# Hybrid decoder layer: one pipeline per kind of attention head beside the block products, operands fetched a head ahead, other homes for raw weights

## The chip, the core and the metric

The kernel runs on one core of a Trainium2 chip. The metric is the device time of one execution in microseconds; the time before is the median of 3 runs. The core's engines are named as in the profile: PE (TensorE matmul; PEld is its weight load), DVE (VectorE), ACT (ScalarE), POOL (GpSimd) and SP (SyncE, which here only issues DMAs). Each engine works through its own instructions in order and waits on semaphores for the others.

## The reference

One decoder layer over 512 tokens of width 2048, all in float32:

```python
h = rmsnorm(x, attn_pre_norm[l])
proj = h @ w_in
gq, gk, gv, gg, ga, dq, dk, dv = [proj[..., int(offs[i]):int(offs[i + 1])]
                                  for i in range(len(IN_SPLITS))]
log_a = jax.nn.log_sigmoid((ga @ w_alpha_up + b_alpha).astype(jnp.float32)) / GLA_TAU
o_a = gla_chunked(gq, gk, gv, log_a)
o_a = rmsnorm(o_a, gla_norm) * silu(gg)
o_b = diff_attention(dq, dk, dv, lam)
o_b = rmsnorm(o_b, diff_norm) * (1.0 - lambda_init)
m = jnp.concatenate([o_a, o_b], axis=-1) @ w_o
x = x + rmsnorm(m, attn_post_norm[l])
h = rmsnorm(x, ffn_pre_norm[l])
f = conv_ffn(h, w_ffn_in[l], conv_w[l], conv_b[l], w_ffn_out[l])
x = x + rmsnorm(f, ffn_post_norm[l])
```

(The shapes of the heads are left out.) There are 4 gated-linear-attention heads (GLA, keys 128 wide, values 256), whose forget gate goes through a product of rank 16, and 4 differential-attention heads (diff: two softmaxes over 128-wide queries and keys, the second subtracted, values 256 wide). Then come w_o and a gated MLP of width 5632 with a depthwise convolution.

## The kernel before

**Products.** Each float32 factor is split in a high half (fp32r) and a low rest: `granule` (L128) takes 4 x 128 rows by 256 columns of weights from `raw`, ACT copies the high half into `ring` (L137) and DVE subtracts it for the low half (L138). A product then takes three matmuls, high by high, high by low, low by high. The normalised input stands in SBUF as `ah` and `al`. `ring` has three slots; a slot's two halves lie at offsets from `place_w`: `APART` for turned units, `APART_N` for units that aren't turned. Here they differ in the low half:

```python
LEVEL, APART, APART_N = (0, 0), (16, 112), (112, 16)
```

**Input projection.** gv's first half, gq's and gk's first half are plain products (`proj_n`, L191 to L193, and `proj_t`, L173 to L175, 512 columns moving). The other columns go in ten units (`InUnit`), each a 2 x 2 block product that saves one of eight block products by adding blocks beforehand. A unit has seven segments x0, z0, y0, z1, x1, y1, y2, of two granules with 24 matmuls of 256 columns each, 336 in all; a turned unit (queries and keys) has the weights stationary (L695 to L697), the others (values, gates) have the sums stationary (L699 to L701). The left factors are blocks of the input (a11, a12, a22) and four sums of blocks (s5, s2, s3, s7) in two halves, which `in_sums` makes with 1024-wide DVE instructions (L402 to L418) and splits (ACT L150, DVE L151). s7 goes into the room of a block of `ah`/`al` that is no longer needed, so it is split only behind the last plain product. The raw weight blocks are added by accumulating DMAs on POOL's queue (`more`) or by DVE (L720). t, the block that x0 starts with, comes into `raw` (4 buffers); b22 comes into `wide` (2 buffers, shared with the sums' temporaries q and r).

**Attention beside it.** Heads are Python generators in the list `fill`. After each granule, `step()` takes `pace` steps of the first generator; what it issues there stands behind that granule's matmuls in PE's order. Each head is a generator of its own; it begins with its DMAs from DRAM, where the units put queries, keys and values. Diff heads have stages for each block of 128 queries: `probs` (scores L589, softmax on DVE and ACT L591 to L605), `turn` (transposes L612, copy aT L614), `values` (L620, norm L623 to L626), `store` (transposes L632, copy dst L634, DMA to `dstd`). A stage runs one block behind the one before it, and a head runs NT + 3 = 7 steps, so the pipeline empties at each head's end. What the heads wrote comes back as `dt` (`place_diff`, split at L150/L151) and, gated, as `ogt` (`turn_gate`, transposes L781) to be w_o's left factor. The forget gate (L422 to L466: load gar, split gas, products L439/L440, L448, Abs, Exp, Ln, scan) feeds the GLA heads.

**Order.** A scheduler sets each engine's order from the order of the program and the buffers, which is why a step that moves in the program moves on all engines. In the last unit `drain()` runs what is left of `fill` in one go:

```python
        else:
            drain()
            place_diff(0)
            u.x1()
```

Of the kernel before, what the change touches and what calls it, by code (L numbers as in the profile page):

```python
# [9 lines left out]
F32 = mybir.dt.float32  # L10
# [25 lines left out]
def hybrid_layer(ctx: ExitStack, tc: tile.TileContext, x, attn_pre_norm, w_in, w_alpha_up, b_alpha,  # L36
# [351 lines left out]

    s7raw = []

    def in_sums():
        for i in range(2):
            def blk(r, c):
                return [v[:, 2 * r + i, HK * c:HK * (c + 1), :].bitcast(F32) for v in (ah, al)]

            a11, a12, a21, a22 = blk(0, 0), blk(0, 1), blk(1, 0), blk(1, 1)

            def flat(name):
                return wide(name).rearrange("p (k c) -> p k c", c=P)
# [10 lines left out]
            yield  # L410
            tt(q, q, a12[0], ALU.add)
            tt(q, q, a12[1], ALU.add)
            split(sums["s3"][0][:, i], sums["s3"][1][:, i], q)
            yield
            r = flat("r")
            tt(r, a11[0], a21[0], ALU.subtract)
            tt(r, r, a11[1], ALU.add)
            tt(r, r, a21[1], ALU.subtract)  # L418
            s7raw.append(r)
            yield  # L420

    def forget_gate():  # L422
        gar = quarter("gar").rearrange("p (k r) -> p k r", r=RANK)
        dma(gar, w_in3[:, :, C_GA:C_GA + RANK])
# [12 lines left out]
        gav = gab[:80, :].rearrange("p (t c) -> p t c", c=P)  # L437
        for k in range(KT):
            mm(gav, gas[:, k, :], ah[:, :, k, :], start=k == 0, stop=False)  # L439
            mm(gav, gas[:, k, :], al[:, :, k, :], start=False, stop=k == KT - 1)  # L440
        gaT = block_tile("gaT")[:80, :]
        nc.vector.tensor_copy(gaT, gab[:80, :])
        yield

        za, bt = [], []
        for h in range(GH):
            zb = bank()
            mm(zb, wup[:, h * P:(h + 1) * P], gaT, start=True, stop=True)  # L448
            bcol = cols[:, h:h + 1]
            za.append(qk_tile("za"))  # L450
            bt.append(tmp("bt"))
            act(za[h], zb, AF.Abs, bias=bcol)
            ts(bt[h], zb, bcol, 0.0, ALU.add, ALU.min)
            if h % 2:
                yield
        for m in za:
            act(m, m, AF.Exp, scale=-1.0)
        for m in za:
            act(m, m, AF.Ln, bias=1.0)
        yield  # L460
        for h, m in enumerate(za):
            tt(m, bt[h], m, ALU.subtract)
            nc.vector.tensor_tensor_scan(bt[h], keep, m, 0.0, ALU.mult, ALU.add)
            dma(bcd[h], bt[h])
            if h % 2:
                yield  # L466


    def gla_head(h):
        q, k, b = (qk_tile(n) for n in ("gq", "gk", "gb"))  # L470
        dma(q, gqd[h // 2][:, h % 2, :])
        dma(k, gkd[h // 2][:, h % 2, :])
        dma(b, bcd[h])
# [4 lines left out]
        yield  # L478
        bc = b.rearrange("p (c x) -> p c x", c=4)
        v = "p (n x) -> p n x"  # L480
        sc = mx.tile([P, 4, P], F32, name="sc", tag="qk", bufs=4)
# [49 lines left out]
            nc.tensor.transpose(kb[:, c * P:(c + 1) * P], kd[:, c * P:(c + 1) * P], ident)  # L531
        kT = tmp("kT")
        act(kT[:, :3 * P], kb[:, :3 * P], AF.Copy)
        yield
        st = None
        for c in range(4):
# [22 lines left out]


    SC = DQK ** -0.5
    dd = []

    def diff_head(h):
        if not dd:
            dist = mx.tile([P, S], F32, name="dist", tag="md", bufs=1)
            nc.gpsimd.iota(dist, [[-1, S]], base=S - P, channel_multiplier=1, allow_small_or_imprecise_dtypes=True)
            nc.gpsimd.affine_select(dist, dist, [[-1, S]], ALU.is_ge, 1e34, base=S - P, channel_multiplier=1)
            dnb = mx.tile([P, DDV], F32, name="dnb", tag="nb", bufs=1)
            bcast_row(dnb, diff_norm[0])  # L570
            ts(dnb, dnb, 1.0 - LAMBDA_INIT, None, ALU.mult)
            dd.extend((dist, dnb))
        dist, dnb = dd
        q, k = ([qk_tile(n) for _ in range(2)] for n in ("dq", "dk"))
        for i in range(2):
            dma(q[i], dqd[h][:, i, :])
            dma(k[i], dkd[h][:, i, :])
        slope = 2.0 ** (-8.0 * (h + 1) / DH)
        e0 = (h % 2) * DDV
        vt = mx.tile([P, NT, DDV], F32, name="dvt", tag="v", bufs=1)  # L580
        dma(vt, dvd[h // 2][:, :, e0:e0 + DDV])
        yield

        def probs(qb):
            nk = (qb + 1) * P
            ps, ls = [], []
            for c in range(2):
# [17 lines left out]
            stt(ps[0][:, :nk], ps[0][:, :nk], ls[0], ps[1][:, :nk], ALU.mult, ALU.subtract)  # L605
            return ps[0]

        def turn(qb, p):
            nk = (qb + 1) * P
            tb = bank()  # L610
            for j in range(qb + 1):
                nc.tensor.transpose(tb[:, j * P:(j + 1) * P], p[:, j * P:(j + 1) * P], ident)  # L612
            aT = tmp("aT")
            act(aT[:, :nk], tb[:, :nk], AF.Copy)  # L614
            return aT

        def values(qb, aT):
            po = bank()
            for j in range(qb + 1):
                mm(po[:, :DDV], aT[:, j * P:(j + 1) * P], vt[:, j, :], start=j == 0, stop=j == qb)  # L620
# [5 lines left out]
            stt(on, po[:, :DDV], r, dnb, ALU.mult, ALU.mult)  # L626
            return on

        def store(qb, on):
            ob = bank()  # L630
            for j in range(2):
                nc.tensor.transpose(ob[:, j * P:(j + 1) * P], on[:, j * P:(j + 1) * P], ident)  # L632
# [3 lines left out]

        stages = (store, values, turn)
        held = [None] * 3
        for i in range(NT + 3):
            for j, f in enumerate(stages):  # L640
                qb = i - 3 + j
                if 0 <= qb < NT:
                    r = f(qb, held[j])
                    if j:
                        held[j - 1] = r
            if i < NT:
                held[2] = probs(i)
            yield


# [3 lines left out]
        return v.rearrange("p (n x) -> p n x", n=2)  # L654

    class InUnit:
        def __init__(self, turned, cols, done):
            self.turned, self.cols, self.done = turned, cols, done
            self.banks = {}

        def block(self, i, j, g):
            return w_in3[:, HK * i + 4 * g:HK * i + 4 * g + 4, self.cols[j]:self.cols[j] + 256]

        def load(self, i, j, alloc=None):
            got = []
            for g in range(2):
                if alloc is None:
                    got.append(load(self.block(i, j, g), 4))
                else:
                    got.append(alloc("b22"))  # L670
                    dma(got[g].rearrange("p (a b) -> p a b", a=4), self.block(i, j, g))
            return got

        def more(self, raws, i, j):
# [139 lines left out]
    after = {1: [lambda: gla_head(2), lambda: gla_head(3)]}  # L814
    for g in range(2):
        units.append(rows_unit(C_DV + 512 * g, dvd[g]))
        for h in (2 * g, 2 * g + 1):
            after[len(units)] = [lambda h=h: diff_head(h)]
# [14 lines left out]
        step()  # L833
    for n in range(2):
        plain_out(gkd)(n, banks[n])
    for i, r in enumerate(s7raw):
        split(sums["s7"][0][:, i], sums["s7"][1][:, i], r)
    fill.extend((gla_head(0), gla_head(1)))
    pace[:] = 0.62, 0.0
    units[0].z0()  # L840
    for i, u in enumerate(units):
        u.y0()
        u.z1()
        if i < len(units) - 1:
            u.x1()
            u.y1()
            units[i + 1].x0()
            u.y2()
            for f in after.get(i, ()):
                fill.append(f())  # L850
# [739 lines left out]
```

## Time and profile before

| | us |
|---|---|
| median of 3 runs | 2122.19 (2121.78 to 2122.52) |
| profiled execution | 2123.57 |
| its span in the trace | 2121.9 |
| PE busy in the span | 2071.5 (98%) |
| DVE busy | 1539.2 (73%) |
| ACT busy | 988.8 (47%) |

The granted clock of PE was 0.994 on the mean. All of the change acts on the first 670 us; from there to the end run w_o and the MLP. The prediction shows the lines on which it rests. In a row of waits the columns are engine, tile and line that waited, what it waited for, then us in total, times and the longest. In a row of a timeline they are start, duration, engine, line, operation, out<-in, shapes, and in brackets the idle time before the row and who ended it.

### The profile page before, as it was taken

The page shows a single profiled execution, that of the slowest core. Times are in us where ns is not written, and L with a number is a line of the kernel's source. Part 1 is how long each engine was busy: PE and PEld are TensorE (multiplying, and loading weights), DVE is VectorE, ACT ScalarE, POOL GpSimd, SP SyncE. Part 2 cuts the span into 40 slices and gives each one's busy share as a digit, 9 for nine tenths or more (in the row PEclk, how much of TensorE's full clock was granted, in tenths as well). Part 3 has the DMA queues.
Part 4 walks back from the last instruction along what each step waited for, and adds up shares of the span by engine and source line. Part 5 has one row for each costly group of instructions (what it writes and reads, how often), then busy time and mean ns, then how long its engine had stood idle before and what let it go on. Part 6 is the DMA issues. An engine that isn't in the chain of part 4 may idle for free.

```text
span 2121.9 us, 35562 instructions
## 1 busy us (share of the span) xinstructions
PE 2071.5 (98%) x14449; PEld 1907.2 (90%) x14449; DVE 1539.2 (73%) x1844; ACT 988.8 (47%) x1274; POOL 287.8 (14%) x306
## 2 busy tenths in 40 slices
PE   7999999999989999999999999999999999999998
PEld 6789999999967889899999999999999878787886
DVE  5867676666754246787786787878777778888887
ACT  4364444455653234344554544454444554444433
POOL 0212122222200000011111111111110110110100
PEclk9999999999999999999999999999999999999999
DMA  5567877898755345356757667577676876676653
GB/s 208 132 166 180 191 180 181 178 197 198 177 161 185 102 145 171 122 126 158 176 135 191 152 152 189 137 169 179 145 168 176 222 223 175 182 188 165 171 164 142
DMA packets 280697, 358.61 MB, mean 169 GB/s; under 512 B 14592, under 2 KB 221876, under 8 KB 278612
## 3 DMA queue, kind: packets, MB, share of 16 engines
q1 hardware_dynamic: 195732, 261.95, 36.6%
q0 software_dynamic: 84800, 94.38, 29.4%
q8 instruction: 113, 1.85, 0.4%
q14 instruction: 52, 0.43, 0.1%
HBM read 311.72 MB, written 44.56 MB: 168 GB/s over the span
## 4 chain that ended last, share of the span: by engine, by line
issue 54%; PE 34%; POOL 4%; DVE 3%; ACT 2%; DMA 2%; POOLq 0%; SPq 0%; DVEq 0%; ACTq 0%
PE bank L695 3%; PE bank L697 3%; PE bank L696 3%; PE bank L192 3%; PE bank L191 3%; PE bank L193 3%; PE bank L699 3%; PE bank L701 3%; PE bank L700 3%; POOL rt L1118 2%; POOL raw L1118 2%; PE bank L502 1%; DVE ring L138 1%; PE bank L589 1%; PE bank L175 1%
## 5 line engine op out<-in xcount | busy, mean ns | idle before, releaser
L137 ACT ACTIVATE ring<-raw 128x1024 fp32r<-128x1024 f32 x325 | 343.7, 1060 | 538.8 <-PE bank L1171 116.1
L138 DVE TENSOR_TENSOR ring<-raw,ring 128x1024 fp32r<-128x1024 f32 x325 | 395.6, 1221 | 230.9 <-ACT ring L137 230.7
L1172 PE MATMUL bank<-ah,ring 128*128 128x256 f32 x1280 | 353.5, 276 | 0.7 <-DVE ring L138 0.7
L1170 PE MATMUL bank<-ah,ring 128*128 128x256 f32 x1280 | 353.3, 276 | 0.0
L1171 PE MATMUL bank<-al,ring 128*128 128x256 f32 x1280 | 353.3, 276 | 0.0
L137 ACT ACTIVATE ring<-rt 128x1024 fp32r<-128x1024 f32 x221 | 233.0, 1059 | 226.8 <-PE bank L1171 143.8
L138 DVE TENSOR_TENSOR ring<-rt,ring 128x1024 fp32r<-128x1024 f32 x221 | 268.8, 1220 | 90.2 <-ACT ring L137 90.0
L1172 PEld LDWEIGHTS bank<-ah,ring 128*128 128x128 f32 x1280 | 240.2, 188 | 0.9 <-DVE ring L138 0.9
L1170 PEld LDWEIGHTS bank<-ah,ring 128*128 128x128 f32 x1280 | 240.2, 188 | 0.1
L1171 PEld LDWEIGHTS bank<-al,ring 128*128 128x128 f32 x1280 | 240.2, 188 | 0.1
L1273 PE MATMUL bank<-ring,ah 128*128 128x512 f32 x424 | 166.6, 393 | 4.3 <-DVE ring L138 4.2
L1274 PE MATMUL bank<-ring,al 128*128 128x512 f32 x424 | 165.2, 390 | 0.0
L1272 PE MATMUL bank<-ring,ah 128*128 128x512 f32 x424 | 159.0, 392 | 2.0 <-ACT ring L137 1.2
L191 PE MATMUL bank<-ring,ah 128*128 128x512 f32 x280 | 110.1, 399 | 4.0 <-ACT ah L150 3.9
L192 PE MATMUL bank<-ring,ah 128*128 128x512 f32 x280 | 110.5, 396 | 0.4 <-DVE ring L138 0.4
L193 PE MATMUL bank<-ring,al 128*128 128x512 f32 x280 | 108.1, 394 | 0.0
L1118 POOL DMA_DIRECT2D raw<-in_w_ffn_in_dram x40 | 51.0, 1278 | 405.4 <-DVE ring L138 402.5
L1273 PEld LDWEIGHTS bank<-ring,ah 128*128 128x128 f32 x424 | 79.6, 188 | 25.5 <-DVE ring L138 9.4
L1272 PEld LDWEIGHTS bank<-ring,ah 128*128 128x128 f32 x424 | 79.3, 188 | 21.6 <-ACT ring L137 4.9
L1118 POOL DMA_DIRECT2D rt<-in_w_ffn_in_dram x40 | 50.9, 1274 | 320.1 <-DVE ring L138 258.4
L1274 PEld LDWEIGHTS bank<-ring,al 128*128 128x128 f32 x424 | 79.6, 188 | 16.3
L695 PE MATMUL bank<-ah,ring 128*128 128x256 f32 x320 | 91.4, 285 | 0.0
(348 smaller groups left out, 5680.7 us busy)
## 6 DMA issues: line engine op xcount, KB each, us to landing
raw<-in_w_ffn_in_dram SPq DMA_DIRECT2D x96, 512.0 KB, 5.4
raw<-in_w_in_dram SPq DMA_DIRECT2D x56, 512.0 KB, 5.8
raw<-in_w_ffn_out_dram SPq DMA_DIRECT2D x48, 512.0 KB, 5.9
raw<-in_w_in_dram POOLq DMA_DIRECT2D x40, 512.0 KB, 6.7
rt<-in_w_ffn_in_dram SPq DMA_DIRECT2D x40, 512.0 KB, 6.1
rt<-in_w_ffn_in_dram POOLq DMA_DIRECT2D x40, 512.0 KB, 6.1
raw<-in_w_ffn_in_dram POOLq DMA_DIRECT2D x40, 512.0 KB, 7.7
raw<-in_w_o_dram SPq DMA_DIRECT2D x32, 512.0 KB, 4.0
```

The source lines that it names most:

```text
L137: act(hi, raw, AF.Copy)
L138: tt(lo, raw, hi.bitcast(F32), ALU.subtract)
L191: mm(banks[t], ah[:, t, s, :], w[0][:, k, :], start=st, stop=False)
L192: mm(banks[t], ah[:, t, s, :], w[1][:, k, :], start=False, stop=False)
L193: mm(banks[t], al[:, t, s, :], w[0][:, k, :], start=False, stop=sp)
L1118: nc.gpsimd.dma_start(out=raws[g].rearrange("p (a b) -> p a b", a=self.a), in_=self.block(0, j, g), accum_op=ALU.add)
L1170: mm(o, wh, sh[:, :, kk, :], start=start and kk == 0 and n == 0, stop=False, **NOW)
L1171: mm(o, wh, sl[:, :, kk, :], start=False, stop=False, **NOW)
L1172: mm(o, wl, sh[:, :, kk, :], start=False, stop=kk == HK - 1, **NOW)
L1272: mm(b[j], sh[:, o:o + P], w[0][:, q, :], start=start and st == 0, stop=False, **NOW)
L1273: mm(b[j], sh[:, o:o + P], w[1][:, q, :], start=False, stop=False, **NOW)
L1274: mm(b[j], sl[:, o:o + P], w[0][:, q, :], start=False, stop=st == 3, **NOW)
```

## The change

1. `in_sums` is cut in `first_sums` (s5, s2) and `last_sums` (s3, s7), and the forget gate stands ahead of both, with `pace` 1.6 rather than 1.35. s7's split moves behind unit 0's z0. The gate's Exp and Ln work on two 1024-wide tiles (`wide`) rather than four of 512.
2. All heads of a kind are one generator (`gla_heads`, `diff_heads`). `there` says how many heads have their operands in DRAM. The next head's queries and keys are fetched ahead (GLA: after kT; diff: at the third block), the diff heads' values at the second block, and the diff pipeline no longer empties between heads: 4 steps a head and 3 at the end. `pace` for the heads is 0.65 rather than 0.62, and holds only from the end of unit 0's z1. `drain()` is gone: all heads have to be through before the last unit's x1.
3. Even units load b21, odd units t, into `wide`; b22 goes into `raw`.
4. `APART_N` has the low half at 112, like the high half.

```diff
-    LEVEL, APART, APART_N = (0, 0), (16, 112), (112, 16)
+    LEVEL, APART, APART_N = (0, 0), (16, 112), (112, 112)
...
-    def in_sums():
+    def first_sums():
         for i in range(2):
...
             split(sums["s2"][0][:, i], sums["s2"][1][:, i], q)
+            s3raw.append(q)
             yield
+
+    def last_sums():
+        for i, q in enumerate(s3raw):
+            a11, a12, a21, a22 = in_blocks(i)
             tt(q, q, a12[0], ALU.add)
             tt(q, q, a12[1], ALU.add)
             split(sums["s3"][0][:, i], sums["s3"][1][:, i], q)
...
-        za, bt = [], []
+        zs = [wide("za") for _ in range(2)]
+        za, bt = [z[:, h * S:(h + 1) * S] for z in zs for h in range(2)], []
...
-        for m in za:
-            act(m, m, AF.Exp, scale=-1.0)
-        for m in za:
-            act(m, m, AF.Ln, bias=1.0)
+        for z in zs:
+            act(z, z, AF.Exp, scale=-1.0)
+        for z in zs:
+            act(z, z, AF.Ln, bias=1.0)
...
+    def gla_heads():
+        got = [None]
+
+        def fetch(h):
+            got[0] = [qk_tile(n) for n in ("gq", "gk", "gb")]
+            for v, src in zip(got[0], (gqd[h // 2][:, h % 2, :], gkd[h // 2][:, h % 2, :], bcd[h])):
+                dma(v, src)
+
+        for h in range(GH):
+            while there["gla"] <= h:
+                yield
+            if got[0] is None:
+                fetch(h)
+                yield
+            yield from gla_head(h, *got[0], got, fetch)
...
+        N = DH * NT
+        fetch_v(0)
+        for i in range(N + 3):
+            h = i // NT
+            if i < N and i % NT == 0:
+                while there["diff"] <= h:
+                    yield
+                if h not in qs:
+                    fetch(h)
+                    yield
             for j, f in enumerate(stages):
-                qb = i - 3 + j
-                if 0 <= qb < NT:
-                    r = f(qb, held[j])
+                n = i - 3 + j
+                if 0 <= n < N:
+                    r = f(n, held[j])
                     if j:
                         held[j - 1] = r
-            if i < NT:
+            if i < N:
                 held[2] = probs(i)
+                if i % NT == 3 and h + 1 < there["diff"]:
+                    fetch(h + 1)
+                if i % NT == 1 and i > NT:
+                    fetch_v(h)
             yield
...
+                if (i, j) == ((0, 0) if self.odd else (1, 0)):
+                    got.append(wide("wt"))
+                    dma(got[g].rearrange("p (a b) -> p a b", a=4), self.block(i, j, g))
+                else:
                     got.append(load(self.block(i, j, g), 4))
...
-            self.b22 = self.load(1, 1, wide)
+            self.b22 = self.load(1, 1)
...
-    fill.extend((in_sums(), forget_gate()))
-    pace[0] = 1.35
+    fill.extend((forget_gate(), first_sums(), last_sums()))
+    pace[0] = 1.6
...
+    there["gla"] = 2
+    fill.extend((gla_heads(), diff_heads()))
+    units[0].z0()
     for i, r in enumerate(s7raw):
         split(sums["s7"][0][:, i], sums["s7"][1][:, i], r)
-    fill.extend((gla_head(0), gla_head(1)))
-    pace[:] = 0.62, 0.0
-    units[0].z0()
     for i, u in enumerate(units):
         u.y0()
         u.z1()
+        pace[0] = 0.65
...
-            drain()
+            assert not fill
             place_diff(0)
```

How this moves instructions shows best in the engines' orders. First DVE around unit 0's z0 and y0 (raw is its t there, `L138` the low halves; `L720` in the kernel before and `L764` in the changed one are the same addition of b22). Before:

```order
L463 SCALAR_TENSOR_TENSOR bt<-keep,za 128x512 x2
L138 TENSOR_TENSOR ring<-raw,ring 128x1024
L151 TENSOR_TENSOR al<-r,ah 128x1024 x2
L138 TENSOR_TENSOR ring<-raw,ring 128x1024 x2
L720 TENSOR_TENSOR raw<-raw,b_1120 128x1024
L138 TENSOR_TENSOR ring<-raw,ring 128x1024
L720 TENSOR_TENSOR raw<-raw,b_1122 128x1024
L138 TENSOR_TENSOR ring<-raw,ring 128x1024
L489 TENSOR_TENSOR d<-gb 128x4x64
```

Now:

```order
L138 TENSOR_TENSOR ring<-raw,ring 128x1024
L423 TENSOR_TENSOR r<-ah 128x1024
L419 TENSOR_TENSOR q<-q,al 128x1024
L764 TENSOR_TENSOR raw<-raw 128x1024
L424 TENSOR_TENSOR r<-r,al 128x1024
L138 TENSOR_TENSOR ring<-raw,ring 128x1024
L151 TENSOR_TENSOR in_s3l<-q,in_s3h 128x1024
L425 TENSOR_TENSOR r<-r,al 128x1024
L764 TENSOR_TENSOR raw<-raw 128x1024
L423 TENSOR_TENSOR r<-ah 128x1024
L138 TENSOR_TENSOR ring<-raw,ring 128x1024
```

The three low halves of the second fence are those of z0's two granules and of y0's first. The sums for s3 (q) and s7 (r), which were all made before, and s7's split, which stood ahead of z0, now lie among and behind these granules.

Second PE behind and in the last unit. `L612`, `L620`, `L632`, `L589` of the kernel before are `L637`, `L646`, `L659`, `L614` of the changed one: transposes of p, value matmuls, transposes of the result, scores. Before, behind the last unit's y0 and z1:

```order
L701 MATMUL bank<-ring,ah 128x256
L632 MATMUL bank<-ident,on 128x128 x2
L589 MATMUL bank<-dk,dq 128x128 x2
L612 MATMUL bank<-ident,s 128x128
L589 MATMUL bank<-dk,dq 128x256 x2
L620 MATMUL bank<-dvt,aT 128x256
L612 MATMUL bank<-ident,s 128x128 x2
L589 MATMUL bank<-dk,dq 128x384 x2
L632 MATMUL bank<-ident,on 128x128 x2
L620 MATMUL bank<-dvt,aT 128x256 x2
L612 MATMUL bank<-ident,s 128x128 x3
L589 MATMUL bank<-dk,dq 128x512 x2
```

Now, the last of the head:

```order
L743 MATMUL bank<-ring,ah 128x256
L744 MATMUL bank<-ring,al 128x256
L745 MATMUL bank<-ring,ah 128x256
L637 MATMUL bank<-ident,s 128x128 x4
L659 MATMUL bank<-ident,on 128x128 x2
L646 MATMUL bank<-dvt,aT 128x256 x4
L659 MATMUL bank<-ident,on 128x128 x2
L743 MATMUL bank<-ring,ah 128x256
L744 MATMUL bank<-ring,al 128x256
L745 MATMUL bank<-ring,ah 128x256
```

The head's last turn now stands with unit matmuls on both sides: 37 lie between its last but one value matmuls and this turn, 25 behind it until the first transposes of `ogt` (L825, before L781), and another 71 until w_o's products.

Third ACT at the same place (L622, L629, L639, L649, L661 are the softmax's exponential, its rescaling, aT, the square for the norm and dst; L811 the gate's sigmoid):

```order
L661 ACTIVATE dst<-bank 128x256
L811 ACT_TABLE_LOAD
L811 ACTIVATE sg<-u_5840 128x512
L649 ACTIVATE jk,ss<-bank 128x256
L622 ACT_TABLE_LOAD
L622 ACTIVATE s,l<-s,nm 128x384 x2
L137 ACTIVATE ring<-raw 128x1024
L629 ACTIVATE s<-s,r_5914 128x384
```
```order
L150 ACTIVATE ah<-dt 128x2x2x128
L622 ACTIVATE s,l<-s,nm 128x512
L150 ACTIVATE ah<-dt 128x2x2x128 x2
L649 ACTIVATE jk,ss<-bank 128x256
L622 ACTIVATE s,l<-s,nm 128x512
L137 ACTIVATE ring<-raw 128x1024
L150 ACTIVATE ah<-dt 128x2x2x128
L629 ACTIVATE s<-s,r_6033 128x512
```

The gates' sigmoids, each with a table load, and the splits of dt (tokens 0 to 255 of the diff heads) lie among the last head's steps, where before the drained head stood ahead of most of them.

More of the change, by code (lines that the diff above doesn't have):

```diff
@@ L389, in hybrid_layer, with flat, in_blocks @@
     s7raw = []
-    def in_sums():
-        for i in range(2):
[L393 to L399, printed above, removed]
+    def flat(name):
+        return wide(name).rearrange("p (k c) -> p k c", c=P)
+    def in_blocks(i):
+        return [[v[:, 2 * r + i, HK * c:HK * (c + 1), :].bitcast(F32) for v in (ah, al)]
+                for r in range(2) for c in range(2)]
+    s3raw = []
+    def first_sums():
+        for i in range(2):
+            a11, a12, a21, a22 = in_blocks(i)
             q = flat("q")
@@ L466, in forget_gate, with gla_head @@
                 yield
[L469 to L473, printed above, removed]
+    there = {"gla": 0, "diff": 0}
+    def gla_heads():
[11 more added lines that the diff above has]
+            yield from gla_head(h, *got[0], got, fetch)
+    def gla_head(h, q, k, b, got, fetch):
         e0 = (h % 2) * GDV
@@ L533, in gla_head @@
         act(kT[:, :3 * P], kb[:, :3 * P], AF.Copy)
+        got[0] = None
+        if h + 1 < there["gla"]:
+            fetch(h + 1)
         yield
@@ L606, in probs, with turn @@
             return ps[0]
-        def turn(qb, p):
-            nk = (qb + 1) * P
+        def turn(n, p):
+            nk = (n % NT + 1) * P
             tb = bank()
-            for j in range(qb + 1):
+            for j in range(nk // P):
                 nc.tensor.transpose(tb[:, j * P:(j + 1) * P], p[:, j * P:(j + 1) * P], ident)
@@ L656, in hybrid_layer @@
     class InUnit:
+        count = 0
         def __init__(self, turned, cols, done):
@@ L813, in hybrid_layer @@
     units = [rows_unit(C_GV + 512, gvd[1]), pair_unit(C_GQ + 256, C_GK + 256, gqd[1], gkd[1])]
-    after = {1: [lambda: gla_head(2), lambda: gla_head(3)]}
+    after = {1: ("gla", 4)}
     for g in range(2):
@@ L848, in hybrid_layer @@
             u.y2()
-            for f in after.get(i, ()):
-                fill.append(f())
+            if i in after:
+                there[after[i][0]] = after[i][1]
             units[i + 1].z0()
         else:
-            drain()
+            assert not fill
             place_diff(0)
```

65 lines of the change are left out of this document (32 added, 33 removed).

## The prediction

> **What bounds the kernel now.** I read the page first, then the waits of TensorE (PE) over the 800 us that hold the attention part, then busy time by stretch, then PE's rows around each hole.
>
> ```profile
> PE 2071.5 (98%) x14449; PEld 1907.2 (90%) x14449; DVE 1539.2 (73%) x1844; ACT 988.8 (47%) x1274; POOL 287.8 (14%) x306
> ```
>
> PE is the bound, so only PE's holes can be won, and its rate. The changed code runs between about 60 and 670 us; there PE waited for these:
>
> ```profile
> PE bank L612 <- DVE s L605: 9.6, 4, 4.2
> PE bank L191 <- ACT ah L150: 3.9, 2, 3.5
> PE bank L192 <- DVE ring L138: 0.4, 1, 0.4
> ```
>
> The busy time by stretch (sum, then PE, PEld, DVE, ACT, POOL, the granted clock, the DMA share and GB/s) says where there is none:
>
> ```profile
> 160.00:580.00 420.00, 420.00 (x3477) 412.73 (x3475) 289.25 (x457) 210.23 (x333) 98.06 (x108) 1.00 0.84 187
> 600.00:650.00 50.00, 40.37 (x167) 30.39 (x166) 29.52 (x65) 25.90 (x58) 3.82 (x8) 0.90 0.40 124
> ```
>
> From 160 to 580 PE is busy without a hole at clock 1.00: seven of the eight attention heads and most of the ten units of block products, all hidden. Fetching their operands earlier cannot win anything there. What is open are two places. The first is early, PE's timeline between unit 0's first granules:
>
> ```profile
> 117.31 0.28 PE L701 MATMUL bank<-ring,ah 128*128 128x256 f32 x1
> 119.45 0.74 PE L173 MATMUL bank<-ah,ring 128*128 128x512 f32 x1 [1.86 <-ACT ring L137]
> ...
> 122.67 0.80 PE L175 MATMUL bank<-ah,ring 128*128 128x512 f32 x1 [2.06 <-DVE ring L138]
> 123.27 0.63 PE L173 MATMUL bank<-ah,ring 128*128 128x512 f32 x1
> ...
> 126.25 0.44 PE L174 MATMUL bank<-al,ring 128*128 128x512 f32 x1
> ...
> 133.61 0.39 PE L173 MATMUL bank<-ah,ring 128*128 128x512 f32 x1
> ...
> 134.97 0.28 PE L699 MATMUL bank<-ring,in_s5h 128*128 128x256 f32 x1
> ```
>
> Six matmuls of 512 take 1.36 us from 133.61 to 134.97, .227 each. From 117.31 to 126.25 there start eleven matmuls, worth about 2.4 us, in 8.94 us: 6.5 us, and with the .4 of the L192 row above **6.9 us lost**. About 2 of these are clock: from 123.27 to 126.25 seven steps take .43 each and not .227.
>
> The second place is the last attention head, which the old schedule drains alone, after the unit's matmuls are gone:
>
> ```profile
> 599.30 0.44 PE L632 MATMUL bank<-ident,on 128*128 128x128 f32 x2
> ...
> 604.41 0.47 PE L612 MATMUL bank<-ident,s 128*128 128x128 f32 x1 [4.23 <-DVE s L605]
> ...
> 610.44 2.16 PE L589 MATMUL bank<-dk,dq 128*128 128x384 f32 x4
> ...
> 616.57 0.55 PE L612 MATMUL bank<-ident,s 128*128 128x128 f32 x3 [1.91 <-DVE s L605]
> 616.95 2.70 PE L589 MATMUL bank<-dk,dq 128*128 128x512 f32 x4
> ...
> 621.72 0.55 PE L191 MATMUL bank<-ring,ah 128*128 128x512 f32 x1
> ```
>
> From 599.30 to 621.72 are 22.4 us. The head's matmuls fill 13.6 of them at half the pace that they have beside units (the granted clock is .90 over a stretch of which most runs at 1), so their work is worth some 6.8: **15.6 us lost**. Another 7.0 go at the start of w_o's products (PE's row and ACT's):
>
> ```profile
> 655.87 0.80 PE L191 MATMUL bank<-ring,ah 128*128 128x512 f32 x1 [3.52 <-ACT ah L150]
> ```
> ```profile
> 655.18 0.63 ACT L150 ACTIVATE ah<-dt 128x512 fp32r<-128x512 f32 x1 [7.52 <-DMA dt<-dstd]
> ```
>
> 3.5 for the last head's output, written to DRAM and read back (dstd, dt), the rest slow clock behind it. In all some 29 us are there to be won, 1.4% of the span.
>
> **The change, part by part.** *The late end.* The diff heads now run as one pipeline that crosses head borders, and the last one lies between the last unit's matmuls, as the order shows. Both losses (15.6 + 7.0 = 22.6) go as they stand: behind the head's last turn, 96 unit matmuls (11 us), the gate's transposes and 37 matmuls of w_o (8.4) now cover the round trip through dstd. What is late next are the head's chains, since few unit matmuls are left for them. Their lengths, from the first score matmul to the end of the p that PE turns (DVE rows):
>
> ```profile
> 615.90 0.62 DVE L605 SCALAR_TENSOR_TENSOR s<-s,rl 128x384 f32<-128x384 f32 x1 [0.74 <-ACT s L604]
> ...
> 628.46 0.75 DVE L605 SCALAR_TENSOR_TENSOR s<-s,rl 128x512 f32<-128x512 f32 x1
> ```
>
> 610.44 to 616.5 is 6.1 us for 384 wide, 616.95 to 629.2 is 12.3 for 512, the latter with splits of dt (L150, waiting for their DMA) in ACT's queue. PE's and ACT's new orders give the covers, at .118 a unit matmul: (1) 512 wide: 14 + 37 unit matmuls and three value matmuls, 7.2 us, against 9.4 to 12.3, since again a split of dt stands ahead of the second half's rescaling in ACT's queue: I take 3.6. (2) 384 wide: cover 43 matmuls and small ones, 6.2 us, against 6.1 plus two table loads, of which ACT's rows say
>
> ```profile
> L767 ACT ACT_TABLE_LOAD x2 | 2.6, 1283 | 0.0
> ```
>
> that they take 1.28 each: 2.4. (3) The first, 128 wide, .6; the copy aT behind the second turn, .6. (4) At the very end the last four value matmuls and the two transposes of their result (`on`) stand next to each other with nothing between. The result passes ACT, POOL and DVE on the way:
>
> ```profile
> 594.44 1.89 PE L620 MATMUL bank<-dvt,aT 128*128 128x256 f32 x8
> 599.30 0.33 PE L632 MATMUL bank<-ident,on 128*128 128x128 f32 x1
> ```
>
> 594.44 + 1.89 to 599.30, about 3.0 to 3.3: I take 3.3. (5) Slow clock after three of these stalls, 2 us each at the early place, where two stalls shared it; with 128-wide work partly running in the slow time, 3.5 in all. Sum 3.6 + 2.4 + .6 + .6 + 3.3 + 3.5 = 14.0, so **−8.6** against 22.6. Bounds: if the chains find their cover and only (4) stays with its clock, −18; if (1) takes 12.3 − 7.2 = 5.1, (2) the whole 2.6 + 1.3, and every stall draws its 2 us of clock, −3.
>
> [...] The row at 119.45 shows the half rate already behind 1.86 us of waiting, so I go by the row.
>
> *The early end.* The forget gate comes first now, the sums s5 and s2 later, s3 and s7 behind them, and s7's split lies behind unit 0's z0. No DVE instruction goes away; PE gets its transposes earlier, the sums come later, so their 1024-wide work meets the first units' granules. Durations (DVE's groups from 60 to 180; the second fence is of DVE's timeline):
>
> ```profile
> L138 DVE TENSOR_TENSOR ring<-raw,ring 128x1024 fp32r<-128x1024 f32 x23 | 27.9, 1221 | 4.8 <-ACT ring L137 4.7
> L463 DVE TENSOR_TENSOR_SCAN bt<-keep,za 128x512 f32<-128x512 f32 x4 | 4.8, 1214 | 0.0
> L489 DVE TENSOR_TENSOR d<-gb 128x256 f32<-128x256 f32 x7 | 2.9, 419 | 1.2 <-DMA gb<-bcd 1.2
> L412 DVE TENSOR_TENSOR q<-q,al 128x1024 f32<-128x1024 f32 x2 | 2.4, 1222 | 0.0
> ```
> ```profile
> 595.16 0.69 DVE L769 TENSOR_TENSOR u<-u,op 128x512 f32<-128x512 f32 x1 [0.29 <-DMA op<-oad]
> 595.77 0.68 DVE L768 TENSOR_TENSOR u<-u,sg 128x512 f32<-128x512 f32 x1
> ```
>
> In the new order DVE has 98 rows from the first bt of the forget gate to unit 1's first lo half: 18 L138 and 30 sums and splits of 1024 at 1.22 (58.6), 4 scans at 1.21 (4.8), 13 of 512 at .69 (9.0), 33 of 256 at .42 to .49 (14.4): 86.8 us. PE from the same point to the same granule has 174 matmuls of 512 at .227 (39.5), 288 of the unit at .118 (34.0) and some 16 small ones (3): 76.5. So DVE becomes the bound there and PE loses about 10.3. The .08 by which back-to-back rows overlap (595.16 + .69 against 595.77) would take 98 × .06, some 6, off; DVE's waits would put some back on:
>
> ```profile
> DVE za L462 <- ACT za L459: 4.8, 3, 1.9
> ```
>
> I let these two cancel. Exp and Ln now take two 1024-wide instructions each and three table loads, not five: 2.6 us less in ACT, which shortens this wait and nothing else. The forget gate's matmuls now stand right behind L381/L383; gar's load moves up nine places on SP, before it was
>
> ```profile
> 62.83 1.57 SPq L102 DMA_DIRECT2D raw<-in_w_in_dram  x2
> ...
> 70.93 0.38 SPq L48 DMA_DIRECT2D gar<-in_w_in_dram  x1
> ```
>
> so it goes out at about 64.4, behind the first, and its split ends about a microsecond after PE asks: +.7. Early total 11.0 after against 6.9 before: **+4.1**; bounds −2 (full overlap, no waits) to +8.5 (no overlap, the 4.8 in full).
>
> *The middle.* A head's dvt has one buffer and is fetched when the head before is through with it, one step (6.2 us at pace .65) ahead of its first use. It moves 512 KB, as the raw weights do:
>
> ```profile
> raw<-in_w_in_dram SPq DMA_DIRECT2D x56, 512.0 KB, 5.8
> ```
>
> 5.8 against 6.2, at three borders: +1.0; bounds 0 and +4 (one in two lost by 2 us, with clock). The raw weights' new homes (b21 or the t block in `wide`) change no count; unit 0's b21 waits for s7's split, which is in the early sum.
>
> *Lo half at 112.* In units that aren't turned, one of three matmuls streams a lo half, now at offset 112 like the hi half. First and last of 105 rows of such a unit, and of 72 of a turned one:
>
> ```profile
> 547.85 0.28 PE L699 MATMUL bank<-ring,ah 128*128 128x256 f32 x1
> ...
> 560.10 0.28 PE L701 MATMUL bank<-ring,in_s2h 128*128 128x256 f32 x1
> ```
> ```profile
> 444.00 0.28 PE L696 MATMUL bank<-al,ring 128*128 128x256 f32 x1
> ...
> 452.09 0.28 PE L695 MATMUL bank<-ah,ring 128*128 128x256 f32 x1
> ```
>
> .1178 against .1139. If the third that moves took the turned rate, 560 × .0039 = 2.2 would go; if nothing, 0. I take **−1.1**; bounds −6.5 (all three follow) and +6.5 (its mirror).
>
> Sum: −8.6 + 4.1 + 1.0 − 1.1 = −4.6; the span 2121.9 becomes 2117.3. The profiled execution took 2123.57, the median of the runs is 2122.19, .3 over its span: **2117.6 us**.
>
> **Rivals.** *A, DVE keeps up early.* If rows overlap and ACT's shorter chain lets DVE run without a pause, the early loss falls to some 5 (−2), and if ACT, off the same load, brings the late stalls to 9.6 (−13): 2121.9 − 2 − 13 − 1 = 2106. For it: DVE was busy only 73% of the whole. Against it: the sums don't go away, and in-order DVE can't run ahead of a granule whose ring slot isn't free. .22. *B, DVE's backlog in units 0 and 1 decides.* A granule gives DVE 24 × .118 = 2.8 us on PE, and five 1024-wide rows, 6.1 us, stand between the lo halves of z0 and y0. If each of the first eight such granules stalls PE by 2 to 3 us (3.3 at most by those rows) and the clock stays low among them, 23 us go, 16 more than before; with −8 at the late end and −1 for the offsets 2122 + 16 − 8 − 1 = 2129. It decides from the point where the early loss is over 15.5, the 6.9 of before and the 8.6 that the late end brings. Against it: the two granules of gk, 24 × .227 = 5.4 us each, stand ahead of z0 and let DVE catch up. .28. *C, the exposed head only moves.* Each chain of the last head is longer than its cover by what it waited before, and PE stands as long inside the unit as it stood behind it: the late loss is some 19, not 14, and the time 2121.9 − 4 + 4 − 1 = 2121. The wait of 4.23 is for it, the 96 unit matmuls behind the last turn against it. .12.
>
> **How the numbers follow.** Forecast .38 (its own range 2113 to 2122), A .22, B .28, C .12. A measurement of this kernel can tell about .2%, 4.2 us: faster is below 2117.9, slower above 2126.4. Faster: half the forecast (.21), all of A: .43. Slower: nearly all of B and a little of the forecast: .28. Same: the rest, .29. The range goes from 2105 (A) to 2130 (B).
>
> **What would show it.** Right: no L612-type wait of 4 us behind the last unit matmul, no dt wait of 7 us at w_o; DVE near 9 tenths from 85 to 165, PE waits for L138 of unit 0's y0 and y1 of 2 to 3 us; waits of 2 to 4 at the last head's turns. Wrong: PE without a hole from 130 to 170 (then A), more than 16 us of holes there (B), L700-type steps that are slower than .118, or new holes at head borders from 220 to 580.

## The result, and the profile after

The changed kernel took 2118.66 us (median of 12 runs), the one before 2122.36 beside it: a ratio of 0.9985, 95% interval 0.9976 to 0.9995, so 1 to 5 us less. In a second series (label e9 below) the ratio was 0.9978, 0.9968 to 0.9988. Forecast were 2117.6 and some 4.6 us less. The profiled execution took 2118.62, its span is 2116.9, 5.0 below the span before. Absolute times belong to their series: the kernel before stands at 2122 beside the changed kernel and at 2128 to 2129 beside the experiments, so what follows compares ratios within a series.

The total is as forecast, but **not by the forecast's terms**. The waits of PE over the first 800 us, for the changed kernel (left out are 11.1 us for L158, which the kernel before has too, and one wait of 0.5):

```profile
PE bank L743 <- ACT u L759: 4.4, 1, 4.4
PE bank L659 <- DVE on L652: 2.8, 1, 2.8
PE bank L637 <- DVE s L630: 2.7, 2, 2.2
PE bank L743 <- DVE u L784: 1.9, 1, 1.9
PE bank L745 <- DVE ring L138: 1.6, 1, 1.6
PE bank L614 <- DMA dk<-dkd: 1.4, 1, 1.4
PE bank L743 <- ACT ring L137: 1.2, 1, 1.2
PE bank L743 <- ACT u L768: 1.2, 1, 1.2
```

The two long ones of before (9.6 for `s`, 3.5 for `ah`) and the two of the early hole are gone, and these eight others have come. Busy time by stretch says where. First the kernel before, then the changed one; the columns are those of the prediction, the third from the end the granted clock:

```profile
100.00:175.00 75.00, 71.08 (x486) 64.48 (x485) 54.08 (x76) 43.20 (x54) 8.91 (x7) 0.95 0.70 166
175.00:560.00 385.00, 385.00 (x3192) 378.52 (x3191) 264.61 (x409) 187.81 (x297) 90.06 (x100) 1.00 0.83 186
560.00:660.00 100.00, 86.01 (x487) 72.11 (x486) 58.95 (x120) 54.63 (x109) 11.67 (x19) 0.93 0.56 153
```
```profile
100.00:175.00 75.00, 72.17 (x526) 67.91 (x525) 70.28 (x94) 37.65 (x47) 10.34 (x8) 1.00 0.75 171
175.00:560.00 385.00, 383.63 (x3163) 374.79 (x3162) 266.34 (x428) 191.97 (x317) 92.21 (x104) 1.00 0.82 186
560.00:660.00 100.00, 86.49 (x503) 76.66 (x503) 56.42 (x98) 48.57 (x87) 10.43 (x14) 0.91 0.66 197
```

From 560 to 660 PE stands idle 13.5 us where it stood 14.0, at a clock of .91 and not .93: nothing has been won there, where the forecast had most of its gain. Early the clock is full and 1.1 us less idle. DVE is at 70.3 of 75, as forecast, and hardly costs PE anything. A point that stands before any head's work, with 541 matmuls ahead of it in both kernels, makes it plainer: the first matmul of unit 0's z0 is at 134.97 before, and now

```profile
128.06 0.28 PE L743 MATMUL bank<-ring,in_s5h 128*128 128x256 f32 x1
```

so **6.9 us are won before 128 us**, the whole early hole. From there on the changed kernel loses some of that again: 3 in unit 0 (1.64 and 1.19 of waits), 1.4 in the middle (a diff head's keys, dk, arrive late once), and at the end no less than before; only the rate of the units that aren't turned gives something back.

### The profile page after: what moved, and what is told of

The parts are those of the page before. It is cut to its first block, busy times and chain, and to the rows that moved or that the text cites. A ratio compares the mean times of both kernels' runs of the same rounds, so it can differ in the third digit from the quotient of the medians.

```text
span 2116.9 us, 35567 instructions
## 1 busy us (share of the span) xinstructions
PE 2067.5 (98%) x14449; PEld 1908.2 (90%) x14449; DVE 1535.6 (73%) x1844; ACT 981.3 (46%) x1264; POOL 283.3 (13%) x306
## 4 chain that ended last, share of the span: by engine, by line
PE 48%; issue 41%; POOL 3%; DVE 3%; DMA 3%; ACT 1%; POOLq 0%; SPq 0%; DVEq 0%; ACTq 0%
PE bank L192 3%; PE bank L193 3%; PE bank L191 3%; PE bank L739 3%; PE bank L741 3%; PE bank L740 3%; PE bank L743 3%; PE bank L745 3%; PE bank L744 3%; PE bank L1217 2%; PE bank L1216 2%; PE bank L1215 2%; PE bank L175 2%; PE bank L174 2%; PE bank L173 2%
## 5 line engine op out<-in xcount | busy, mean ns | idle before, releaser
L137 ACT ACTIVATE ring<-raw 128x1024 fp32r<-128x1024 f32 x315 | 333.2, 1060 | 523.8 <-PE bank L1216 113.1
L138 DVE TENSOR_TENSOR ring<-raw,ring 128x1024 fp32r<-128x1024 f32 x315 | 383.9, 1221 | 243.2 <-ACT ring L137 241.2
L1217 PE MATMUL bank<-ah,ring 128*128 128x256 f32 x1280 | 354.1, 277 | 1.7 <-DVE ring L138 1.7
L1215 PE MATMUL bank<-ah,ring 128*128 128x256 f32 x1280 | 353.4, 276 | 0.0
L137 ACT ACTIVATE ring<-rt 128x1024 fp32r<-128x1024 f32 x221 | 233.2, 1059 | 223.1 <-PE bank L1216 139.6
L138 DVE TENSOR_TENSOR ring<-rt,ring 128x1024 fp32r<-128x1024 f32 x221 | 269.0, 1221 | 89.4 <-ACT ring L137 87.3
L192 PE MATMUL bank<-ring,ah 128*128 128x512 f32 x280 | 109.8, 393 | 0.0
L743 PE MATMUL bank<-ring,ah 128*128 128x256 f32 x320 | 93.6, 293 | 4.3 <-DVE u L784 1.9
```

What stands on the lines that cost most here:

```text
L137: act(hi, raw, AF.Copy)
L138: tt(lo, raw, hi.bitcast(F32), ALU.subtract)
L192: mm(banks[t], ah[:, t, s, :], w[1][:, k, :], start=False, stop=False)
L743: mm(o, sh[:, n, kk, :], wh[:, k, :], start=st, stop=False, **NOW)
L1215: mm(o, wh, sh[:, :, kk, :], start=start and kk == 0 and n == 0, stop=False, **NOW)
L1217: mm(o, wl, sh[:, :, kk, :], start=False, stop=kk == HK - 1, **NOW)
```

## The experiments

Each is compared with the kernel before in the same series. The changed kernel's own ratio is .9985 or .9978 (.998 from here on, some 4 us).

**e1 and e2, the low half's offset.** e1 sets it back in the changed kernel, e2 makes this one edit in the kernel before:

```diff
-    LEVEL, APART, APART_N = (0, 0), (16, 112), (112, 112)
+    LEVEL, APART, APART_N = (0, 0), (16, 112), (112, 16)
```

> The changed kernel with the low half of units that aren't turned back at offset 16. Theory (the offset sets the rate of these units): start-to-start step of their matmuls back from .1161 to .1178 us, 1680 of them, so 2.9 us more than the changed kernel, the rest of the trace unchanged. Rival (the rate came from something else, such as the raw blocks' new homes): the step stays at .116 and the time does not move.

> The kernel before with nothing but the low half at 112. Theory: 2.9 us less than before (2119.4), step .116. Rival: step .1178, no change.

Ratios: e1 .9996 (.9983 to 1.0009), e2 .9988 (.9975 to 1.0001). Both lean the way of the theory, by 2.5 to 3.5 us, and neither interval settles it alone. The steps do: the mean over some 1500 pairs of neighbouring starts is .1178 before and .1177 in e1, .1161 in the changed kernel and .1160 in e2. All other traces agree: with the low half at 112 the mean lies at .1155 to .1163 in ten runs, with it at 16 at .1178 in four. So the offset decides whether the rate moves, and 1680 × .0017 = 2.9 us; how far it moves differs by run, and why was not tried. The mean hides two rates, seen in e2 at the first and last row of 74 and of 105 neighbouring matmuls:

```profile
134.95 0.28 PE L699 MATMUL bank<-ring,in_s5h 128*128 128x256 f32 x1
...
143.54 0.28 PE L700 MATMUL bank<-ring,in_s2l 128*128 128x256 f32 x1
...
547.39 0.28 PE L699 MATMUL bank<-ring,ah 128*128 128x256 f32 x1
...
559.18 0.28 PE L701 MATMUL bank<-ring,in_s2h 128*128 128x256 f32 x1
```

8.59/73 = .1177 in the one, 11.79/104 = .1134 in the other: where the fast rate holds, all three matmuls of a group have it and not only the one whose operand moved. In the kernel before no granule has it: their means lie at .1173 to .1180. What decides which granules get it was not tried.

**e3, the order of the first fillers.** The changed kernel with sums first, gate last:

```diff
-    fill.extend((forget_gate(), first_sums(), last_sums()))
-    pace[0] = 1.6
+    fill.extend((first_sums(), last_sums(), forget_gate()))
+    pace[0] = 1.35
```

> The changed kernel with the old order of the first fillers (sums first, forget gate last, pace 1.35). Theory (the early hole was the gate's burst standing among the last granules of gk, with nothing left to hide it): PE again waits 3 to 5 us between 100 and 130 with slow clock behind, 3 to 7 us more than the changed kernel. Rival (the amount of work on DVE decides, whichever order): no waits before 130 and within 1.5 us of the changed kernel, or faster, since the sums are ready sooner.

The theory fell. The ratio is .9971 (.9958 to .9984), not slower than the changed kernel, and between 95 and 175 PE's one wait is

```profile
PE bank L745 <- DVE ring L138: 0.8, 1, 0.8
```

With wide tiles, then, the order isn't what closes the hole. The kernel before shows the other candidate, in ACT's timeline ahead of the high half that gk's third granule waited for:

```profile
106.55 1.28 ACT L459 ACT_TABLE_LOAD   x1
...
116.00 1.28 ACT L459 ACT_TABLE_LOAD   x1
...
118.35 1.04 ACT L137 ACTIVATE ring<-raw 128x1024 fp32r<-128x1024 f32 x1
```

Exp (L457) and Ln (L459) of the gate's four tiles alternate from 104.61 on, each change loads a table, five times up to 116.00, and L137 stands behind all of it.

**e5 and e6, the wide tiles.** e5 is e3 with the four 512-wide tiles back; e6 is the kernel before with nothing but the two wide ones:

```diff
-        za, bt = [], []
+        zs = [wide("za") for _ in range(2)]
+        za, bt = [z[:, h * S:(h + 1) * S] for z in zs for h in range(2)], []
...
-        for m in za:
-            act(m, m, AF.Exp, scale=-1.0)
-        for m in za:
-            act(m, m, AF.Ln, bias=1.0)
+        for z in zs:
+            act(z, z, AF.Exp, scale=-1.0)
+        for z in zs:
+            act(z, z, AF.Ln, bias=1.0)
```

> The changed kernel with the forget gate last and its Exp and Ln on four 512-wide tiles, as before. Theory (the early hole was ACT's: five table loads and twelve small activations of the gate in one stretch ahead of the high halves of gk): PE waits for L137 and L138 between 105 and 130 again, 4 to 7 us of holes with the slow clock behind them, DVE less than 40 of 50 us busy there. Rival (the new start of the attention or the later split of s7 closed it): no wait over 1 us before 130, as with the gate last and wide tiles.

> The kernel before with nothing but the gate's two 1024-wide tiles. Theory: the waits for L173 and L175 at 117 to 127 go, 4 to 7 us less than before. Rival (wide tiles alone do nothing, order and attention's start count): both waits stay, within 1.5 us of before.

e5: ratio .9993 (.9978 to 1.0007); between 95 and 175 PE waits as before:

```profile
PE bank L175 <- DVE ring L138: 2.5, 1, 2.5
PE bank L173 <- ACT ring L137: 1.2, 1, 1.2
```

e6: ratio .9964 (.9952 to .9977), and both are gone:

```profile
PE bank L701 <- DVE ring L138: 2.4, 2, 1.7
PE bank L699 <- ACT ring L137: 0.7, 2, 0.5
```

The first matmul of z0, in e5 and then in e6:

```profile
134.29 0.28 PE L743 MATMUL bank<-ring,in_s5h 128*128 128x256 f32 x1
```
```profile
128.44 0.28 PE L699 MATMUL bank<-ring,in_s5h 128*128 128x256 f32 x1
```

With the gate last and narrow tiles it stands at 134 to 135, with wide ones at 128, in the kernel before as in the changed one. That one edit closes the hole there, and by itself (e6) it does at least as much as the whole change. Not all of this gain is placed: of the 6.5 us at z0, e6 loses 3.1 again by waits in unit 0, and its span, 2119.2, lies only 2.7 below the one before, which was traced in another series.

How the tiles do it shows in ACT's timeline of e6, at the same place:

```profile
111.87 1.06 ACT L137 ACTIVATE ring<-raw 128x1024 fp32r<-128x1024 f32 x1 [7.84 <-PE bank L174]
112.84 1.99 ACT L150 ACTIVATE ah<-r 128x1024 fp32r<-128x1024 f32 x2
...
115.78 2.40 ACT L452 ACTIVATE za<-bank,cols 128x512 f32<-128x512 f32 x4
...
121.53 1.28 ACT L459 ACT_TABLE_LOAD   x1
```

The copy for gk's third granule now starts at 111.87, as soon as PE has left its slot in `ring`, and the gate's work on ACT begins behind it, at 115.78 rather than at 104.61. By the program the two `wide` buffers hold s7's raw sums (r) until these are split (the L150 row, and L151 on DVE), so the gate gets its tiles only then. So the hole closed because the gate left its place ahead of the copy; the loads that the wide tiles save stand behind it now. Whether fewer loads in the old place would have been enough was not tried. In the changed kernel the gate is first in any case: its work on ACT is done by 92.4, ahead of all this, and whether it would have needed the wide tiles was not run either.

**e4, e10, e11, the pace of the heads.** The changed kernel with 0.70, 0.75 and 0.80:

```diff
-        pace[0] = 0.65
+        pace[0] = 0.70
```

> The changed kernel with heads paced at 0.70 steps a granule, not 0.65. Theory (the late loss of about 22 us is one of position: the last head's last steps lie too close together in the last unit): the last steps are 60 to 90 unit matmuls apart, the late holes fall from 22 us to 5 to 9, the time is 2102 to 2107. Rival (its chains on ACT with table loads and splits are too long for any cover, or a faster pace opens holes between 160 and 560): not faster than 2115.

> The changed kernel once more, as the measure for the two runs beside it. Theory: 0.15 to 0.3% below before, with the waits of the first profile at the same instructions (4.4 us for u in the last unit, 2.8 for on, 1.6 for unit 0's low half). Rival (these waits were a chance of one execution): other instructions wait.

> The changed kernel with heads at 0.75 steps a granule. Theory (only the place of the last head's end counts, and with 0.70 a wait of 4.6 us for a high half behind table loads was left): the late holes get no larger than with 0.70, 2098 to 2110 where before is at 2122. Rival (faster steps leave too little cover for each chain): holes of 1 to 3 us at many turns between 200 and 560, slower than 0.70 by 5 us or more.

> The same at 0.80. Theory: the heads then wait for their operands (the last one can't begin before its unit is done), so little changes against 0.75: within 4 us of it. Rival: holes between 200 and 560, slower than the changed kernel.

Ratios: 0.70 .9908 (.989 to .9927); 0.75 .9901 (.9888 to .9914); 0.80 .9964 (.995 to .9978); the changed kernel beside the last two .9978. Against it 0.75 wins another 16 us (.77% of 2123). In the changed kernel the last head's four turns stand 35, 45 and 51 unit matmuls apart, in PE's order, with 96 left behind the last; at 0.70 it is 73, 98 and 81, with 152 left, and at 0.75 it is 74, 71 and 116, with 190 left. The theories of e4 and e10 held, but for one distance outside e4's 60 to 90. The stretch from 560 to 660 at 0.70 and then at 0.75:

```profile
560.00:660.00 100.00, 91.49 (x566) 81.40 (x565) 55.63 (x80) 48.38 (x77) 8.60 (x10) 0.97 0.66 197
```
```profile
560.00:660.00 100.00, 95.08 (x576) 84.06 (x575) 56.05 (x74) 48.83 (x75) 7.94 (x8) 0.97 0.69 207
```

8.5 and 4.9 us of idle PE, not 13.5, at .97 and not .91. From 175 to 560 PE waits for nothing at either pace. Too fast is no good again. At 0.80 the kernel is about as fast as the changed one, not within 4 us of 0.75 as the theory had it: the heads now catch up with their operands, and where they do PE waits, as in the rival's holes. Its waits from 175 to 560 are

```profile
PE bank L614 <- DMA dk<-dkd: 8.2, 5, 2.6
PE bank L646 <- DMA dvt<-dvd: 0.5, 1, 0.5
```

The repeat (e9) waits at the instructions of the first profile (4.3 for `u`, 2.8 for `on`, 1.6 for unit 0's low half), so these waits belong to the program.

**e7, a faster pace without the change.** The kernel before, `pace[:] = 0.72, 0.0` and not 0.62:

> The kernel before with its heads at 0.72 steps a granule, not 0.62. Theory (a head of its own takes 7 or 8 steps of which several are nearly empty, and its chains end in the last unit only because the pace is low): the drained head shrinks, the late loss of 22.6 us falls to below 10, the time 12 to 18 us below before. Rival (the last head's start is set by when its operands are there, or heads that drain one by one stall at each border when they are stepped faster): at most 5 us below before, with holes at head borders or the drain still there.

The theory fell: 1.0033 (1.0018 to 1.0048), slower than before. Its last head still runs through all its own steps, the turns of which stand 56, 43 and 74 unit matmuls apart and end 96 before the end, as in the changed kernel; from 560 to 660 PE is idle for 20.9 us:

```profile
560.00:660.00 100.00, 79.15 (x495) 71.49 (x495) 57.32 (x97) 48.04 (x85) 9.37 (x12) 0.88 0.58 157
```

So a pace of 0.72 is worth nothing without the pipeline of all heads, and the pipeline is worth little at the end without a faster pace. Heads of their own at a still higher pace, which would end as far ahead of the last unit matmul as e10's, were not run, so that the pipeline is needed for this is not shown.

**e8, no operands ahead.** The changed kernel without the two places that fetch the next head's queries and keys:

```diff
-        if h + 1 < there["gla"]:
-            fetch(h + 1)
...
-                if i % NT == 3 and h + 1 < there["diff"]:
-                    fetch(h + 1)
```

> The changed kernel without the operands fetched a head ahead: each head's queries and keys are fetched at its own start, one step before their use. Theory (the stretch from 160 to 560 has cover to spare, fetching ahead wins nothing there): no new holes over 2 us between 200 and 560, and within 2 us of the changed kernel except for what seven more steps push into the last unit. Rival (fetching ahead is what keeps the head borders closed): a wait of 1 to 4 us for dq, dk, gq or gb at most of the six borders, 6 to 15 us more.

.9956 (.9942 to .997), so not slower than the changed kernel, and from 175 to 560 PE's only wait is

```profile
PE bank L644 <- DMA dvt<-dvd: 0.8, 1, 0.8
```

At this pace fetching ahead wins nothing. That the ratio is even lower, by some 5 us, goes with a last head that is moved again by its extra steps (from 560 to 660 a clock of .97 with 13.7 us idle); that it is the cause was not shown.

**e12, what worked, together.** The order of e3 and 0.75:

> The changed kernel with the old order of the first fillers (sums first, forget gate last, pace 1.35) and heads at 0.75. Theory (the wide tiles closed the early hole, the order only moves DVE's load): the waits of 1.6 and 1.2 us in unit 0 shrink to one below 1 us, the rest as with 0.75 alone: 0.5 to 3 us less than it, ratio to before 0.987 to 0.991. Rival (sums first bring the gate's burst into the first unit): new holes between 100 and 175, slower than 0.75 alone.

2103.49 us, ratio .9888 (.9873 to .9903): the lowest of all, some 24 us below before. Between 95 and 560 no wait of PE is over 0.8. It can't be told from 0.75 alone by these intervals.

## Why the prediction came out right, step by step

The total came out right by luck: the late end was forecast 9.9 us too good and the early one 8.0 us too bad, and the two errors nearly cancelled. The working of neither holds as it stands.

*"Early total 11.0 after against 6.9 before: +4.1"* failed; measured are 3 after, so −3.9. (The 6.9 was itself 6.5: the .4 of the L192 row is a wait at 642, in w_o.) Four things in it were off. The main one is the sentence that the wide Exp and Ln mean "2.6 us less in ACT, which shortens this wait and nothing else". The prediction saw L173 wait for ACT and L175 for DVE, and then reckoned on DVE alone; it never asked what stood ahead of that L137 in ACT's queue, which was the gate; with the gate elsewhere the hole is gone. Then, gar's load went out at 62.3, and the gate's matmuls didn't wait at all, where +.7 was taken. Third, DVE did become full, as forecast; behind the scans it has no pause for 71 us:

```profile
90.22 1.20 DVE L138 TENSOR_TENSOR ring<-raw,ring 128x1024 fp32r<-128x1024 f32 x1
...
160.78 0.43 DVE L525 COPY_PREDICATED sc<-masks,bank 128x256 f32<-128x256 uint8 x1
162.94 1.23 DVE L138 TENSOR_TENSOR ring<-wt,ring 128x1024 fp32r<-128x1024 f32 x1 [1.73 <-ACT ring L137]
```

but its 1024-wide rows start 1.137 us apart, not 1.22, and its pauses come to 4.2: the 98 rows from L460 at 81.28 to L138's end at 164.2 took 82.9 us, pauses included, and not 86.8. Last, and this undoes the 10.3, PE itself had more to do: it begins the granule of that L138 only at 166.49, 2.3 us behind DVE, with 82.4 us busy on the way and not 76.5. The gate and the first GLA head have 67 small matmuls there, 7.4 us, where the sum had 16 for 3. So DVE was never what bounded PE over this stretch; it cost the 1.6 of one granule. The bounds given (−2 to +8.5) did not hold −3.9, since both came from DVE.

*"Both losses go as they stand … 14.0, so −8.6"* failed in size: the old losses went, the new ones are as large, which is rival C's mechanism at this end. (The 15.6 is 1.4 too large: the clock granted from 599.30 to 621.72 was .77 and not half, and the 40 matmuls there are worth 8.2 us by the steps that the same shapes have from 430 to 580.) Of the five terms, (1) was right in place, 2.2 measured for 3.6. Of (3), 1.2, came .5 at the second turn, not the first, and .5 for aT behind the fourth. (4) was right in place and too small. PE's timeline:

```profile
579.45 0.28 PE L745 MATMUL bank<-ring,ah 128*128 128x256 f32 x1
584.15 0.58 PE L743 MATMUL bank<-ring,in_s3h 128*128 128x256 f32 x1 [4.42 <-ACT u L759]
...
600.12 0.66 PE L637 MATMUL bank<-ident,s 128*128 128x128 f32 x4 [2.19 <-DVE s L630]
...
601.46 3.50 PE L646 MATMUL bank<-dvt,aT 128*128 128x256 f32 x8 [0.47 <-ACT aT L639]
607.77 0.55 PE L659 MATMUL bank<-ident,on 128*128 128x128 f32 x2 [2.81 <-DVE on L652]
609.50 0.58 PE L743 MATMUL bank<-ring,ah 128*128 128x256 f32 x1 [1.18 <-ACT u L768]
```

From the last values at 601.46 to the next unit matmul at 609.50 go 8 us for work worth about one. (2) was seen at the right engine and the wrong waiter: the two table loads are there, but what stands behind them and is waited for is z0's evacuation L759, which z1 needs, as z1 adds into the same bank. ACT's timeline:

```profile
577.26 1.28 ACT L811 ACT_TABLE_LOAD   x1 [0.53 <-PE bank L646]
...
579.57 1.28 ACT L622 ACT_TABLE_LOAD   x1
...
582.08 1.04 ACT L137 ACTIVATE ring<-raw 128x1024 fp32r<-128x1024 f32 x1
583.02 0.60 ACT L629 ACTIVATE s<-s,r 128x384 f32<-128x384 f32 x1
583.53 0.57 ACT L759 ACTIVATE u<-bank 128x512 f32<-128x512 f32 x1
```

That costs 4.4 us for 2.4. L768 and L784 (1.2 and 1.9), evacuations of the unit's banks too, were not in the sum. The prediction counted the head's own chains and left out the unit's instructions that queue behind them on ACT and DVE. The dt wait at w_o went, as said. e4 and e10 show that all of this hangs on where the last head's steps lie.

*"Lo half at 112: −1.1"* was right in sign and too small; −2.9 measured, by a rate that takes all three matmuls in some granules.

*"The middle: +1.0"* was the right size at another load: 1.4 for dk and not dvt.

Sum of what was measured: −3.9 early, +1.4 in the middle, −2.9 by the rate, and at the end 13.5 + 86.5 × .09 = 21.3 after against 14.0 + 86.0 × .07 = 20.0 before, +1.3: −4.1. At w_o's last matmul the changed kernel's trace is 4.3 ahead (807.79 against 812.08); the other .7 of the 5.0 between the two spans lies behind it, where both run the same program, and e9's trace of the same kernel is 3.1 longer there. So one trace places a term by its waits, but not its last microseconds.

Of the rivals, A's early half came true (by another cause than the one it named) and C's late one; B did not, since DVE's full queue held up only one granule of PE for 1.6 us, and ACT another for 1.2.

## What to carry to other kernels

When PE waits for a short copy, list everything that stands ahead of it in that engine's queue. Here a gate that nobody waited for stood ahead of it with nearly 14 us of work, five table loads among it; two wider tiles, whose buffers came free only later, moved it behind, and that alone brought at least as much as the whole change. Work that is fitted in beside a main stream must end well before the stream does, so set its pace by the distance between its last steps: 0.65 to 0.75 was worth some three and a half times the change (.77% against .22% in one series). And when a tail is moved under cover, price the covering work's own small instructions that then queue behind it.

## What the runs showed of the hardware

PE ran at half its rate behind one short wait and at the full rate behind another. After one of 1.95 us, at 621.42, the next matmuls start .21 apart for 3.6 us, and the granted clock was .50 from 621.61 to 625.03; after one of 1.64, at 139.60, they start .12 apart, and the granted clock was 1.00 from 139.60 to 143.00:

```profile
139.60 0.39 PE L745 MATMUL bank<-ring,in_s2h 128*128 128x256 f32 x1 [1.64 <-DVE ring L138]
139.83 0.28 PE L743 MATMUL bank<-ring,in_s2h 128*128 128x256 f32 x1
...
140.77 0.28 PE L745 MATMUL bank<-ring,in_s2h 128*128 128x256 f32 x1
```
```profile
621.42 0.43 PE L743 MATMUL bank<-ring,ah 128*128 128x256 f32 x1 [1.95 <-DVE u L784]
...
624.85 0.37 PE L744 MATMUL bank<-ring,al 128*128 128x256 f32 x1
625.05 0.28 PE L745 MATMUL bank<-ring,ah 128*128 128x256 f32 x1
```

So the wait of 1.95 us cost 1.7 more here: 17 steps took 3.63 us, where steps of .114, as they are behind 625.05, make 1.94. Why the clock dropped behind the one wait and not behind the other was not shown.
